# Weight halves and memory keys kept in DRAM, and one output projection for two branches

## The chip, the cores and the metric

The kernel runs on one core of one Trainium2 chip. The time is the device time of one execution in microseconds, from three runs of the kernel before. A core has TensorE (PE; its weight loads are shown as PEld), VectorE (DVE), ScalarE (ACT), GpSimd (POOL) and SyncE (SP), which issues every DMA here, in order.

## The reference

A trunk of two residual layers over 2048 tokens of width 1024, float32. Both have one combined input projection, three branches, each times a SiLU gate, and one output projection over the joined branches (512 + 512 + 256 channels):

```python
z = xn @ w_in                       # xn = rms_norm(h, norm_g[layer])
# layer 0 (even): A chunked spatial gating | B multi-scale pooling | M memory attention
# layer 1 (odd):  C window attention       | D convolution module  | M memory attention
y = concatenate([ya, yb, ym], axis=-1) @ w_out_even   # odd: [yc, yd, ym] @ w_out_odd
h = h + y
```

Branch M attends from every token to 256 memory tokens, whose keys and values depend on the layer alone.

## The kernel before

The tokens are four blocks of 512 (`TB`), channels on the 128 partitions. Each block passes the even layer and then the odd one: eight stages, in the order even 0, even 1, odd 0, even 2, odd 1, even 3, odd 2, odd 3. Between the layers the residual rows lie in DRAM (`h1`).

Every float32 matrix product is three matmuls (`mm3`, L125): each factor is split into a high half, rounded to the PE's fast format, and a low half, the rest. `hi_of` (L119) is a copy on ACT, `lo_of` (L122) a subtraction on DVE or POOL; all of them show as L120 and L123, and the tile's name tells which: `wh`, `wl` weights, `xnh`, `xnl` the normalised input, `yh`, `yl` the branch outputs, `km` memory keys, `q` queries, `kt` window keys.

`wslot` (L137) brings 128x1024 weights: SP loads the raw tile (two buffers), ACT makes `wh`, POOL or DVE `wl` (four buffers each). `share` gives DVE every third low half in even stages and none in odd ones. A unit of the input projection (`proj`, L322) is one slot and 24 matmuls. This is done anew in each stage: a weight of a layer is loaded and split four times.

`load_mem` (L427) loads the memory keys in each stage and stacks them (`stack_keys`, L297: four copies on ACT, four low halves on DVE, into `km`). `finish` (L330) splits a branch output, the low half on DVE. `out_steps` (L504) multiplies finished outputs with output weights, one 128-channel unit at a time, and DVE adds each unit to the residual row (L521), which frees the PSUM bank. It is called for the first branch (offset 0, four inputs, 12 matmuls a unit), the second (offset 4, the same) and the memory branch (offset 8, two inputs, 6 matmuls a unit).

`Norm` prepares the next stage's input within this one: sums of squares (`square_sum`, L160: ACT squares, DVE adds), a scale on DVE (L193), and `split`, whose low halves `xnl` DVE makes between the row adds of the last projection. In odd stages the convolution runs on DVE as 31 multiply-adds on each of four tiles (L689), put between other work. `_SEQ` (L945) lists the events of an odd stage: `S`, `V` window attention, `s`, `v` memory attention, `e` finishes branch C, `oN` runs N output units.

The order on each engine is made by a scheduler at build time, which simulates the program; on the chip each engine takes its instructions in that order.

Of the kernel before, what the change touches and what calls it, by code (L numbers as in the profile page):

```python
# [18 lines left out]
P = 128  # L19
# [33 lines left out]
def trunk(ctx: ExitStack, tc: tile.TileContext, x, mem, par, par1, wkv, w_v, w_cm0, w_kvc, w_cm1, w_o0, w_o1, awt, bw, dpw, abse, out):  # L53
# [83 lines left out]
    def wslot(src, n=1024, eng=None):  # L137
        raw = rp.tile([P, 1024], F32, tag="wr", name="wr", bufs=2)[:, :n]
        hi = wp.tile([P, 1024], F32R, tag="wh", name="wh", bufs=4)[:, :n]
        lo = wp.tile([P, 1024], F32R, tag="wl", name="wl", bufs=4)[:, :n]  # L140
        nc.sync.dma_start(raw, src)
        hi_of(hi, raw)
        turns[0] += 1
        lo_of(eng or (V if turns[0] % share[0] == 0 else G), lo, raw, hi)
        return hi, lo
# [14 lines left out]
    def square_sum(srcs, n_buf=1):  # L160
        bufs = []
        for _ in range((n_buf + 2) // 2):
            t = p_tile().rearrange("p a b -> p (a b)")
            bufs += [t[:, :TB], t[:, TB:]]
        total, bufs = bufs[0], bufs[1:]
        for i, src in enumerate(srcs):
            sq = bufs[i % n_buf] if i else total
            A.activation(sq, src, AF.Square)
            if i:
                V.tensor_tensor(total, total, sq, op=ALU.add)  # L170
        return total, bufs[0]
# [40 lines left out]
    mkv = [tc.dram_tile([2, P, TB], F32, name=f"mkv{l}") for l in range(2)]  # L212
# [46 lines left out]
    def prep_mem(memt):  # L259
        for l in range(2):  # L260
            gm = sb.tile([P, P], F32, tag="kn", name="kn", bufs=2)[:, :64]
            V.tensor_tensor(gm, par_of(f"mq{l}"), par_of(f"mk{l}"), op=ALU.mult)
            kv = sb.tile([P, 2, 2, 256], F32, tag="pt", name="kv", bufs=2)
            for hf in range(2):
                ws = [view(wslot(wkv[l, hf, q]), "p (k n) -> p k n", k=4) for q in range(2)]
                for mt in range(2):
                    pb = mm_bank()[:, :256]
                    ms = slice(mt * P, (mt + 1) * P)
                    for k in range(KC):
                        wh, wl = ws[k // 4]  # L270
                        mm3(pb, memt[0][k // 4][:, k % 4, ms], memt[1][k // 4][:, k % 4, ms],
                            wh[:, k % 4, :], wl[:, k % 4, :], k == 0, k == KC - 1)
                    if hf:
                        A.copy(kv[:, 1, mt, :], pb)
                    else:
                        mem_keys(gm, mt, pb, kv[:, 0])
            nc.sync.dma_start(mkv[l].rearrange("a p m -> p a m"), kv.rearrange("p a b m -> p a (b m)"))
# [44 lines left out]
    def proj(xn, w_cm, unit):  # L322
        wh, wl = view(wslot(w_cm[unit]), "p (k c) -> p k c", k=KC)
        pb = mm_bank()
        for k in range(KC):
            mm3(pb, wh[:, k, :], wl[:, k, :], xn[0][:, k, :], xn[1][:, k, :], k == 0, k == KC - 1)
        pump(2)
        return pb

    def finish(y):  # L330
        hi = half("yh", 4, F32R)
        lo = half("yl", 4, F32R)
        done[0] = hi_of(hi, y)
        lo_of(V, lo, y, hi)
# [92 lines left out]
    def load_mem(l):  # L427
        km = sb.tile([P, 4, 2, 256], F32R, tag="km", name="km", bufs=1)
        vm = sb.tile([P, 2, 256], F32, tag="vm", name="vm", bufs=1)
        t = short()[:, :TB]  # L430
        nc.sync.dma_start(t, mkv[l][0])
        nc.sync.dma_start(vm.rearrange("p a b -> p (a b)"), mkv[l][1])
        stack_keys(km, t.rearrange("p (c m) -> p c m", c=2))
        return km, vm

    def memory(l, q, ys, fill):
# [10 lines left out]
        return [finish(y) for y in ys]  # L447
# [3 lines left out]
    class Norm:  # L451
# [30 lines left out]
        def split(self):  # L482
# [21 lines left out]
    def out_steps(st, first, ys):  # L504
# [94 lines left out]
    def even(st, ahead):  # L599
# [119 lines left out]
    def odd(st, ahead):  # L719
# [23 lines left out]
        cq, mq, gc, yc, ym, steps = [], [], [], [], [], []  # L743
# [47 lines left out]
        project_out(st, 8, ym)  # L791
# [6 lines left out]
        project_out(st, 4, yd)  # L798
# [109 lines left out]
    def conv_mix(st, hd, ys):  # L908
        ws = [view(wslot(dpw[q]), "p (k n) -> p k n", k=2) for q in range(2)]
# [14 lines left out]
    first_v = [wslot(w_v[0, 0], eng=G)]  # L924
    lead.measure()
    with behind(ET.DVE):
        first_v.append(wslot(w_v[0, 1], eng=V))
    first_v = [view(w, "p (k n) -> p k n", k=4) for w in first_v]
    xn = lead.scale_split()
    for n, (is_odd, b) in enumerate(order):  # L930
# [15 lines left out]
        "s1 o2 v0 s2 v1 o2 s3 v2 o2 v3")  # L946
# [30 lines left out]
def _lay_out(i):  # L977
# [12 lines left out]
    for n, w in (("w_o0", i["w_out_even"][0]), ("w_o1", i["w_out_odd"][0][rows1])):  # L990
        a[n] = np.concatenate([_out_slots(w[P * k:P * (k + m)], m) for k, m in ((0, 4), (4, 4), (8, 2))])
# [53 lines left out]
```

## Time and profile before

| | us |
|---|---|
| median of three runs (1968.65 to 1969.47) | 1969.15 |
| the profiled execution | 1970.85 |
| its span, first to last instruction | 1968.9 |
| PE busy | 1899.1 |
| DVE busy | 1374.2 |
| POOL busy | 872.8 |
| ACT busy | 825.3 |

The profiled execution has 1.95 us around its span. A busy time is a share of the whole span; what an engine holds up is read from the waits and from stretches of single stages. "Idle before" tells what ended the wait of an engine; matmuls overlap, so a stretch of them is read from the starts.

### The profile page before, as it was taken

To read this page: it belongs to the slowest core of one execution; us is meant where nothing else is said; L and a number is where in the kernel's file an instruction comes from. 1 tells how busy PE (TensorE), PEld (TensorE's weight loads), DVE (VectorE), ACT (ScalarE), POOL (GpSimd) and SP (SyncE) were. 2 spreads that over 40 slices of the span, in tenths; PEclk is the share of its full clock that TensorE was granted. 3 is DMA by queue.
4 is the path that set the end of the run, shared out by engine and by line. 5 is a ranking of instruction groups with operands and counts; after the bars stand their busy time and mean duration, and the time that the engine had idled before them with its cause. 6 is when DMAs were issued, how large, how long until landed. Compare 5 with 4: busy or idle time off the path is not lost.

```text
span 1968.9 us, 26523 instructions
## 1 busy us (share of the span) xinstructions
PE 1899.1 (96%) x10034; PEld 1569.0 (80%) x10034; DVE 1374.2 (70%) x2262; ACT 825.3 (42%) x1663; POOL 872.8 (44%) x593
## 2 busy tenths in 40 slices
PE   6999999999998999999999899999999989999999
PEld 6878888787886878878788687988878767888687
DVE  6776544645999673565699967355569986699954
ACT  4453324423355442442435443353333544435532
POOL 3672225323555443623445443453245544445542
PEclk9999999999999999999999999999999999999999
DMA  5443353334322334232532233432252223532122
GB/s 207 152 137 113 102 173 106 109 99 166 97 86 70 103 107 160 96 113 86 177 97 67 68 124 132 136 113 97 86 178 86 75 66 111 166 108 71 59 76 75
DMA packets 61440, 218.96 MB, mean 111 GB/s; under 512 B 6785, under 2 KB 6913, under 8 KB 61185
## 3 DMA queue, kind: packets, MB, share of 16 engines
q1 hardware_dynamic: 61312, 217.27, 33.9%
q8 instruction: 79, 1.29, 0.3%
q14 instruction: 49, 0.39, 0.1%
HBM read 198.63 MB, written 18.61 MB: 110 GB/s over the span
## 4 chain that ended last, share of the span: by engine, by line
PE 47%; DVE 9%; ACT 1%; issue 0%; DMA 0%; POOL 0%; ACTq 0%; POOLq 0%; SPq 0%
PE mm L126 12%; PE mm L127 12%; PE mm L128 12%; DVE cv L689 3%; PE cv L128 2%; PE cv L126 2%; PE cv L127 2%; DVE xnl L123 1%; PE pv L417 1%; PE tr L385 1%; PE tr L312 1%; PE tr L313 1%; DVE row L521 1%; PE pv L357 1%; DVE pt L853 1%; DVE q L123 0%
## 5 line engine op out<-in xcount | busy, mean ns | idle before, releaser
L123 POOL TENSOR_TENSOR wl<-wr,wh 128x1024 fp32r<-128x1024 f32 (+1 forms) x250 | 606.6, 2428 | 866.6 <-ACT wh L120 808.2
L120 ACT CAST wh<-wr 128x1024 fp32r<-128x1024 f32 (+1 forms) x300 | 312.6, 1042 | 655.0 <-PE mm L127 358.6
L126 PE MATMUL mm<-xnh,wh 128*128 128x512 f32 x1176 | 464.3, 395 | 0.4 <-ACT u L354 0.4
L128 PE MATMUL mm<-xnh,wl 128*128 128x512 f32 x1176 | 461.6, 393 | 0.2 <-DVE wl L123 0.2
L127 PE MATMUL mm<-xnl,wh 128*128 128x512 f32 x1176 | 460.7, 392 | 0.0
L689 DVE SCALAR_TENSOR_TENSOR cv<-hx,dwh,cv 128x512 f32<-128x512 f32 x464 | 349.0, 752 | 9.1
L128 PEld LDWEIGHTS mm<-xnh,wl 128*128 128x128 f32 x1176 | 221.3, 188 | 47.2 <-issue 1.2
L127 PEld LDWEIGHTS mm<-xnl,wh 128*128 128x128 f32 x1176 | 221.6, 188 | 45.9 <-issue 2.8
L126 PEld LDWEIGHTS mm<-xnh,wh 128*128 128x128 f32 x1176 | 221.4, 188 | 44.0 <-issue 0.6
L126 PE MATMUL mm<-yh,wh 128*128 128x512 f32 x534 | 215.5, 406 | 23.8 <-DVE row L521 14.4
L127 PE MATMUL mm<-yl,wh 128*128 128x512 f32 x534 | 210.6, 394 | 1.1 <-DVE yl L123 1.1
L128 PE MATMUL mm<-yh,wl 128*128 128x512 f32 x534 | 210.5, 394 | 0.0
L521 DVE TENSOR_TENSOR row<-mm,row 128x512 f32<-128x512 f32 x160 | 109.1, 686 | 122.9 <-PE mm L128 122.6
L126 PEld LDWEIGHTS mm<-yh,wh 128*128 128x128 f32 x534 | 100.9, 190 | 56.3 <-DVE row L521 23.1
L127 PEld LDWEIGHTS mm<-yl,wh 128*128 128x128 f32 x534 | 101.0, 189 | 21.6 <-DVE yl L123 2.0
L128 PEld LDWEIGHTS mm<-yh,wl 128*128 128x128 f32 x534 | 100.9, 189 | 21.4 <-issue 0.2
L123 DVE TENSOR_TENSOR wl<-wr,wh 128x1024 fp32r<-128x1024 f32 (+1 forms) x50 | 66.3, 1326 | 68.8 <-ACT wh L120 68.7
L403 ACT ACTIVATE p<-tr,mnb,qm 128x256 f32<-128x256 f32 x128 | 70.6, 561 | 69.6 <-DVE mnb L400 65.1
L377 POOL TENSOR_SCALAR p<-p,mrd 128x256 f32<-128x256 f32 x128 | 64.1, 521 | 79.5 <-DVE mrd L406 78.4
L126 PE MATMUL mm<-wh,xnh 128*128 128x256 f32 x320 | 91.8, 287 | 2.9 <-ACT xnh L120 1.8
L128 PE MATMUL mm<-wh,xnl 128*128 128x256 f32 x320 | 91.0, 285 | 1.3 <-DVE xnl L123 1.1
L126 PE MATMUL cv<-xnh,wh 128*128 128x512 f32 x232 | 92.1, 397 | 0.0
(226 smaller groups left out, 3378.3 us busy)
## 6 DMA issues: line engine op xcount, KB each, us to landing
wr<-in_w_cm_dram SPq DMA_DIRECT2D x176, 512.0 KB, 3.5
wr<-in_w_o_dram SPq DMA_DIRECT2D x80, 512.0 KB, 3.5
wr<-in_w_v_dram SPq DMA_DIRECT2D x16, 512.0 KB, 3.5
row<-in_x_dram SPq DMA_DIRECT2D x16, 512.0 KB, 4.1
h<-row SPq DMA_DIRECT2D x16, 512.0 KB, 3.5
row<-h SPq DMA_DIRECT2D x16, 512.0 KB, 3.9
out_dram<-row SPq DMA_DIRECT2D x15, 512.0 KB, 2.7
x<-in_x_dram SPq DMA_DIRECT2D x8, 512.0 KB, 3.6
```

What stands on the lines that cost most here:

```text
L120: return A.copy(hi, raw)
L123: eng.tensor_tensor(lo, raw, hi.bitcast(F32), op=ALU.subtract)
L126: T.matmul(out, lhsT=lh, rhs=rh, start=first, stop=False)
L127: T.matmul(out, lhsT=lh, rhs=rl, start=False, stop=False)
L128: T.matmul(out, lhsT=ll, rhs=rh, start=False, stop=last)
L312: T.matmul(out, lhsT=q[g][:, cols], rhs=keys[:, g], start=True, stop=False)
L313: T.matmul(out, lhsT=q[g][:, cols], rhs=keys[:, 2 + g], start=False, stop=True)
L357: T.matmul(sp[:, 2 * tt:2 * tt + 2], lhsT=sq[:, tt * P:(tt + 1) * P], rhs=par_of("bones"), start=True, stop=True)
L377: G.tensor_scalar(p[:, h, :], p[:, h, :], rd[:, h:h + 1], 1.0, op0=ALU.mult, op1=ALU.mult)
L403: A.activation(p[:, h, :], banks[h // 2][:, (h % 2) * 256:(h % 2) * 256 + 256], AF.Exp, bias=nb[:, h:h + 1], scale=qr[:, tt, h:h + 1], acc ...
L521: add = V.tensor_tensor(row, pb, row, op=ALU.add)
L689: V.scalar_tensor_tensor(dst, src, w, acc, op0=ALU.mult, op1=ALU.add)
```

## The change

`wslot` takes a key. At a key's first use it loads and splits as before, into one tile `w` that holds both halves (four buffers), and SP stores that tile in DRAM. At the second to fourth use SP loads both halves from there (1 MB) and nothing is split. Only the weights of the memory keys and values have no key: they are used once. The stacked keys are made and stored once per layer (`mkey`), and `load_mem` only loads them (1 MB). The low halves in `finish` and `split`, and the adds of `square_sum` (but for the first one of the program), go from DVE to POOL. The memory branch's outputs join the second branch's projection: six inputs, 18 matmuls a unit, slots of 768 columns with one unit each; the projection at offset 8 is gone. In odd stages `_SEQ` has one output unit where it had two, and those left over run after the convolution's norm.

```diff
@@ -134,14 +134,22 @@
 
-    def wslot(src, n=1024, eng=None):
+    halves = {}
+
+    def wslot(src, n=1024, eng=None, key=None):
+        w = wp.tile([P, 2, 1024], F32R, tag="w", name="w", bufs=4)[:, :, :n]
+        hi, lo = w[:, 0], w[:, 1]
+        if key in halves:
+            nc.sync.dma_start(w.bitcast(F32), halves[key])
+            return hi, lo
         raw = rp.tile([P, 1024], F32, tag="wr", name="wr", bufs=2)[:, :n]
-        hi = wp.tile([P, 1024], F32R, tag="wh", name="wh", bufs=4)[:, :n]
-        lo = wp.tile([P, 1024], F32R, tag="wl", name="wl", bufs=4)[:, :n]
         nc.sync.dma_start(raw, src)
...
         lo_of(eng or (V if turns[0] % share[0] == 0 else G), lo, raw, hi)
+        if key:
+            halves[key] = tc.dram_tile([P, 2, n], F32, name="w_" + "_".join(map(str, key)))
+            nc.sync.dma_start(halves[key], w.bitcast(F32))
         return hi, lo
...
@@ -167,7 +175,7 @@
             if i:
-                V.tensor_tensor(total, total, sq, op=ALU.add)
+                (V if n_buf > 1 else G).tensor_tensor(total, total, sq, op=ALU.add)
         return total, bufs[0]
...
@@ -209,7 +217,8 @@
     vtail = const.tile([P, P], F32, name="vtail")
-    mkv = [tc.dram_tile([2, P, TB], F32, name=f"mkv{l}") for l in range(2)]
+    mkey = [tc.dram_tile([P, 4, 2, 256], F32, name=f"mkey{l}") for l in range(2)]
+    mval = [tc.dram_tile([P, TB], F32, name=f"mval{l}") for l in range(2)]
 
...
@@ -274,7 +283,10 @@
                         mem_keys(gm, mt, pb, kv[:, 0])
-            nc.sync.dma_start(mkv[l].rearrange("a p m -> p a m"), kv.rearrange("p a b m -> p a (b m)"))
+            km = sb.tile([P, 4, 2, 256], F32R, tag="km", name="km", bufs=1)
+            stack_keys(km, kv[:, 0])
+            nc.sync.dma_start(mkey[l], km.bitcast(F32))
+            nc.sync.dma_start(mval[l], kv[:, 1].rearrange("p b m -> p (b m)"))
 
...
@@ -320,7 +332,7 @@
     def proj(xn, w_cm, unit):
-        wh, wl = view(wslot(w_cm[unit]), "p (k c) -> p k c", k=KC)
+        wh, wl = view(wslot(w_cm[unit], key=("cm", int(w_cm is w_cm1), unit)), "p (k c) -> p k c", k=KC)
         pb = mm_bank()
...
@@ -328,10 +340,10 @@
     def finish(y):
-        hi = half("yh", 4, F32R)
-        lo = half("yl", 4, F32R)
+        hi = half("yh", 6, F32R)
+        lo = half("yl", 6, F32R)
         done[0] = hi_of(hi, y)
-        lo_of(V, lo, y, hi)
+        lo_of(G, lo, y, hi)
         return hi, lo
...
@@ -427,10 +439,8 @@
         vm = sb.tile([P, 2, 256], F32, tag="vm", name="vm", bufs=1)
-        t = short()[:, :TB]
-        nc.sync.dma_start(t, mkv[l][0])
-        nc.sync.dma_start(vm.rearrange("p a b -> p (a b)"), mkv[l][1])
-        stack_keys(km, t.rearrange("p (c m) -> p c m", c=2))
+        nc.sync.dma_start(km.bitcast(F32), mkey[l])
+        nc.sync.dma_start(vm.rearrange("p a b -> p (a b)"), mval[l])
         return km, vm
...
@@ -485,7 +494,7 @@
                 hi_of(xn[0][:, k, :], self.xs[k])
-                lo_of(V, xn[1][:, k, :], self.xs[k], xn[0][:, k, :])
+                lo_of(G, xn[1][:, k, :], self.xs[k], xn[0][:, k, :])
             rate[0] = 3
...
@@ -506,12 +515,13 @@
         per = KC // n
+        size = per * n * P
         ws = {}
...
             if q not in ws:
-                ws[q] = view(wslot(w_o[first + q]), "p (u k n) -> p u k n", u=per, k=n)
+                ws[q] = view(wslot(w_o[first + q, :, :size], size, key=("o", int(st["odd"]), first + q)), "p (u k n) -> p u k n", u=per, k=n)
             wh, wl = ws[q]
...
@@ -633,14 +643,12 @@
         df = [None] * 4
-        ym = memory(0, q, gm, lambda tt: pool_windows(st, df, tt))
+        memory(0, q, gm, lambda tt: pool_windows(st, df, tt))
         nx = ahead()
-        wb = view(wslot(bw, TB), "p (g d) -> p g d", g=4)
-        yb = [pool_map(st, g, df[g], wb) for g in range(3)]
-        project_out(st, 8, ym)
-        yb.append(pool_map(st, 3, df[3], wb))
+        wb = view(wslot(bw, TB, key=("bw",)), "p (g d) -> p g d", g=4)
+        yb = [pool_map(st, g, df[g], wb) for g in range(4)]
+        steps = out_steps(st, 4, yb + [finish(y) for y in gm])
         ya = [sgu(st, 0, xhs, wt, abias)]
-        steps = out_steps(st, 4, yb)
         for f in steps[:4]:
...
@@ -788,14 +793,16 @@
         hd = conv_swish(st, xhs)
-        project_out(st, 8, ym)
+        for f in steps:
+            f()
+        ym = [finish(y) for y in gm]
         if nx:
...
             st["next"] = nx.split()
-        project_out(st, 4, yd)
+        project_out(st, 4, yd + ym)
         flush()
...
@@ -943,7 +950,7 @@
 _SEQ = ("f6 q S0 g2 S1 g2 V0 f1 S2 V1 f1 S3 V2 f2 s0 V3 f2 e "
-        "s1 o2 v0 s2 v1 o2 s3 v2 o2 v3")
+        "s1 o1 v0 s2 v1 o1 s3 v2 o1 v3")
 _TC = dict(schedule_with_timeline_sim=True)
...
@@ -988,7 +995,7 @@
     for n, w in (("w_o0", i["w_out_even"][0]), ("w_o1", i["w_out_odd"][0][rows1])):
-        a[n] = np.concatenate([_out_slots(w[P * k:P * (k + m)], m) for k, m in ((0, 4), (4, 4), (8, 2))])
+        a[n] = np.concatenate([_out_slots(w[P * k:P * (k + m)], m) for k, m in ((0, 4), (4, 6))])
     a["awt"] = i["a_ws"][0].transpose(2, 0, 1)
...
     a["dpw"] = _tm_slots(i["d_pw"][0], 2)

...
```

VectorE at the end of stage even 2, from the last projection's first row add on (`row`) to the next stage; before, then now:

```order
L521 TENSOR_TENSOR row<-cv,row 128x512
L123 TENSOR_TENSOR xnl<-x,xnh 128x512 x3
L521 TENSOR_TENSOR row<-mm,row 128x512
L123 TENSOR_TENSOR xnl<-x,xnh 128x512
L123 TENSOR_TENSOR xnl<-p,xnh 128x512 x2
L521 TENSOR_TENSOR row<-mm,row 128x512
L123 TENSOR_TENSOR xnl<-p,xnh 128x512 x2
L521 TENSOR_TENSOR row<-cv,row 128x512
L521 TENSOR_TENSOR row<-mm,row 128x512 x2
L521 TENSOR_TENSOR row<-cv,row 128x512
```

```order
L602 TENSOR_TENSOR gt<-u_7894,gt 128x512
L604 SCALAR_TENSOR_TENSOR gt<-cv,gt 128x512
L531 TENSOR_TENSOR row<-mm,row 128x512 x2
L531 TENSOR_TENSOR row<-cv,row 128x512
L531 TENSOR_TENSOR row<-mm,row 128x512 x2
L531 TENSOR_TENSOR row<-cv,row 128x512
L531 TENSOR_TENSOR row<-mm,row 128x512 x2
```

The eight low halves `xnl` have left DVE, and its row adds follow each other. They stand on POOL now, behind the four `yl` of the first branch (`krsb` and `qc` are the next stage's):

```order
L123 TENSOR_TENSOR yl<-gt,yh 128x512 x4
L123 TENSOR_TENSOR xnl<-x,xnh 128x512 x4
L123 TENSOR_TENSOR xnl<-p,xnh 128x512 x4
L165 TENSOR_TENSOR krsb<-krsa,nhalf 128x2 x4
L373 TENSOR_TENSOR qc<-qss,nhalf 128x8 x4
```

GpSimd at the end of the attention of stage odd 1 (`qm` query scales, `p<-p,mrd` the weighing of a memory tile); before, then now:

```order
L361 TENSOR_TENSOR qm<-qss,nhalf 128x8
L123 TENSOR_TENSOR wl<-wr,wh 128x1024
L361 TENSOR_TENSOR qm<-qss,nhalf 128x8
L377 TENSOR_SCALAR p<-p,mrd 128x256 x8
L123 TENSOR_TENSOR wl<-wr,wh 128x1024
L377 TENSOR_SCALAR p<-p,mrd 128x256 x4
L123 TENSOR_TENSOR wl<-wr,wh 128x1024
L377 TENSOR_SCALAR p<-p,mrd 128x256 x4
```

```order
L373 TENSOR_TENSOR qm<-qss,nhalf 128x8
L862 AFFINE_SELECT pt<-pt 128x512
L373 TENSOR_TENSOR qm<-qss,nhalf 128x8
L389 TENSOR_SCALAR p<-p,mrd 128x256 x4
L123 TENSOR_TENSOR yl<-gt,yh 128x512 x4
L389 TENSOR_SCALAR p<-p,mrd 128x256 x12
L178 TENSOR_TENSOR p<-p 128x512
L123 TENSOR_TENSOR yl<-gt,yh 128x512 x2
```

The `wl` rows are gone in this stage, and the four `yl` of branch C stand behind the first weighing and ahead of the other three.

SyncE in stage even 0, from the pooling weights on; before, then now:

```order
L141 DMA wr_1438<-in_bw_dram 128x512
L277 DMA mkv1_106<-kv_853 128x2x512
L141 DMA wr_1444<-in_w_cm0_dram 128x1024
L141 DMA wr_1492<-in_w_cm0_dram 128x1024
L141 DMA wr_1540<-in_w_cm0_dram 128x1024
L141 DMA wr_1588<-in_w_o0_dram 128x1024
```

```order
L146 DMA wr_1448<-in_bw_dram 128x512
L288 DMA mkey1_106<-km_1022 128x2048
L152 DMA w_cm_0_11_1358<-w_1353 128x2048
L146 DMA wr_1455<-in_w_cm0_dram 128x1024
L152 DMA w_bw_1452<-w_1447 256x1x512
L146 DMA wr_1504<-in_w_cm0_dram 128x1024
L442 DMA km_1043<-mkey0_105 128x2048
L152 DMA w_cm_0_12_1459<-w_1454 128x2048
L146 DMA wr_1553<-in_w_cm0_dram 128x1024
L152 DMA w_cm_0_13_1508<-w_1503 128x2048
```

The store of a slot's halves stands between the raw loads, and the reload of the stacked keys behind the second layer's store of them.

## Rows read from the trace of the kernel before

**Rows 1.** The page's first lines: busy us, share of the span, instructions of an engine
```profile
span 1968.9 us, 26523 instructions
...
PE 1899.1 (96%) x10034; PEld 1569.0 (80%) x10034; DVE 1374.2 (70%) x2262; ACT 825.3 (42%) x1663; POOL 872.8 (44%) x593
```

**Rows 2.** TensorE's rate, timeline: start us, duration us; one 24-matmul unit
```profile
500.08 0.39 PE L126 MATMUL mm<-xnh,wh 128*128 128x512 f32 x1
...
505.53 0.39 PE L126 MATMUL mm<-xnh,wh 128*128 128x512 f32 x1
```

**Rows 3.** Waits of TensorE: engine, line, releaser: us in total, times, longest
```profile
PE mm L126 <- DVE row L521: 15.7, 17, 1.6
PE tr L179 <- DVE p L170: 11.1, 1, 11.1
PE mm L126 <- ACT yh L120: 8.5, 4, 3.9
PE pv L862 <- DVE pt L853: 5.0, 3, 2.3
PE tr L714 <- DVE kn L711: 3.7, 5, 0.9
```

**Rows 4.** Granted clock of the core over the span
```profile
core 0: 1968.9 us, clock 0.995
```

**Rows 5.** Four stretches, one per odd stage: us, busy us of each engine, clock, DMA
```profile
600.00:650.00 50.00, 43.91 (x222) 32.00 (x221) 48.58 (x95) 26.92 (x75) 25.38 (x23) 0.93 0.18 58
1075.00:1125.00 50.00, 43.09 (x212) 32.25 (x209) 48.38 (x100) 28.90 (x78) 24.64 (x21) 0.93 0.24 79
1575.00:1600.00 25.00, 19.75 (x91) 14.10 (x89) 22.14 (x41) 9.85 (x26) 11.65 (x9) 0.86 0.16 45
1825.00:1875.00 50.00, 45.39 (x234) 34.77 (x234) 49.15 (x96) 27.20 (x72) 26.09 (x24) 1.00 0.20 64
```

**Rows 6.** Timeline at an even stage's end: VectorE, then TensorE
```profile
945.95 4.09 DVE L123 TENSOR_TENSOR xnl<-x,xnh 128x512 fp32r<-128x512 f32 x3
949.96 0.68 DVE L521 TENSOR_TENSOR row<-mm,row 128x512 f32<-128x512 f32 x1
...
950.69 0.50 PE L126 MATMUL mm<-yh,wh 128*128 128x512 f32 x1 [1.52 <-DVE row L521]
```

**Rows 7.** VectorE's groups by shape: count, busy us, mean ns, idle before
```profile
L521 DVE TENSOR_TENSOR row<-mm,row 128x512 f32<-128x512 f32 x160 | 109.1, 686 | 122.9 <-PE mm L128 122.6
L123 DVE TENSOR_TENSOR yl<-gt,yh 128x512 fp32r<-128x512 f32 x80 | 66.3, 845 | 12.3 <-ACT yh L120 12.3
...
L123 DVE TENSOR_TENSOR km<-u,km 64x512 fp32r<-64x512 f32 x32 | 42.5, 1328 | 2.9 <-ACT km L300 2.2
```

**Rows 8.** Timeline at the end of an odd stage's attention: VectorE, ScalarE, GpSimd, TensorE
```profile
1113.39 3.12 DVE L689 SCALAR_TENSOR_TENSOR cv<-hx,dwh,cv 128x512 f32<-128x512 f32 x4
1116.42 0.15 DVE L400 SCALAR_TENSOR_TENSOR mnb<-mmx,qm 128x4 f32<-128x4 f32 x1
...
1118.79 2.17 ACT L120 CAST yh<-gt 128x512 fp32r<-128x512 f32 x4
...
1119.21 1.85 POOL L377 TENSOR_SCALAR p<-p,mrd 128x256 f32<-128x256 f32 x4 [3.06 <-DVE mrd L406]
...
1119.46 1.22 PE L126 MATMUL mm<-yh,wh 128*128 128x512 f32 x2 [3.91 <-ACT yh L120]
```

**Rows 9.** One line on VectorE: duration ns min/median/max, first and last start
```profile
L123 DVE TENSOR_TENSOR yl<-gt,yh x80: 675/686/2546, 149.3 to 1944.3; 128x512 fp32r<-128x512 f32 x80
```

**Rows 10.** GpSimd's low halves of weights by shape, columns as in rows 7
```profile
L123 POOL TENSOR_TENSOR wl<-wr,wh 128x1024 fp32r<-128x1024 f32 x248 | 604.0, 2437 | 857.5 <-ACT wh L120 799.1 <-PE mm L128 24.3 <-ACT pt L387 11.8
...
L123 POOL TENSOR_TENSOR wl<-wr,wh 128x512 fp32r<-128x512 f32 x2 | 2.6, 1292 | 9.1 <-ACT wh L120 9.1
```

**Rows 11.** ScalarE's high halves of weights, columns as in rows 7
```profile
L120 ACT CAST wh<-wr 128x1024 fp32r<-128x1024 f32 x296 | 310.1, 1048 | 651.2 <-PE mm L127 358.6 <-issue 110.2 <-PE cv L127 66.7
```

**Rows 12.** Issue of weights on SyncE (KB each, us to landing); all loads of L141
```profile
wr<-in_w_cm_dram SPq DMA_DIRECT2D x176, 512.0 KB, 3.5
...
DMA to landing us min/median/max: 2.5/3.5/7.6
```

**Rows 13.** DMA of 0 to 25 us: GB/s in 40 slices
```profile
GB/s 0 0 26 151 249 413 420 406 393 419 413 407 414 413 419 419 439 426 419 419 341 0 0 105 242 387 105 52 85 341 397 432 407 380 351 436 413 426 419 406
```

More of the change, by code (lines that the diff above doesn't have):

```diff
@@ L446, in memory @@
                 fill(tt)
-        return [finish(y) for y in ys]
     paced, rate, done = [], [1], [None]
@@ L609, in even @@
                 with behind(ET.DVE):
-                    ws = [view(wslot(w_v[hf, j]), "p (k n) -> p k n", k=4) for j in range(2)]
+                    ws = [view(wslot(w_v[hf, j], key=("v", hf, j)), "p (k n) -> p k n", k=4) for j in range(2)]
             for tt in range(NT):
@@ L693, in keys @@
         xn, kt, va = st["xn"], st["kt"], st["va"]
-        ws = [view(wslot(w_kvc[q]), "p (k n) -> p k n", k=4) for q in range(2)]
+        ws = [view(wslot(w_kvc[q], key=("kvc", q)), "p (k n) -> p k n", k=4) for q in range(2)]
         for tt in range(NT):
@@ L742, in odd @@
         km, vm = load_mem(1)
-        cq, mq, gc, yc, ym, steps = [], [], [], [], [], []
+        cq, mq, gc, yc, steps = [], [], [], [], []
         pc, pm = {}, {}
@@ L779, in odd @@
         run(len(fills))
-        for f in steps:
-            f()
-        ym = [finish(y) for y in gm]
         gd = [gate(st, w_cm1, 16 + u) for u in range(3)]
@@ L908, in conv_mix @@
     def conv_mix(st, hd, ys):
-        ws = [view(wslot(dpw[q]), "p (k n) -> p k n", k=2) for q in range(2)]
+        ws = [view(wslot(dpw[q], key=("dpw", q)), "p (k n) -> p k n", k=2) for q in range(2)]
         for u in range(4):
@@ L923, in trunk @@
     nc.sync.dma_start(pc, par)
-    first_v = [wslot(w_v[0, 0], eng=G)]
+    first_v = [wslot(w_v[0, 0], eng=G, key=("v", 0, 0))]
     lead.measure()
     with behind(ET.DVE):
-        first_v.append(wslot(w_v[0, 1], eng=V))
+        first_v.append(wslot(w_v[0, 1], eng=V, key=("v", 0, 1)))
     first_v = [view(w, "p (k n) -> p k n", k=4) for w in first_v]
@@ L964, in _out_slots @@
     per = KC // n
-    v = w.reshape(n, P, n, per, P).transpose(2, 1, 3, 0, 4)
-    return np.ascontiguousarray(v).reshape(n, P, D)
+    v = w.reshape(n, P, KC // per, per, P).transpose(2, 1, 3, 0, 4).reshape(KC // per, P, per * n * P)
+    return np.pad(v, ((0, 0), (0, 0), (0, D - v.shape[2])))
 def _chan(v):
```

## The prediction

> **What bounds the kernel.** I read the busy lines first: TensorE works 1899.1 of 1968.9 us, VectorE 1374.2, GpSimd 872.8, ScalarE 825.3 [rows 1]. TensorE is the bound, and 69.8 us is all that it stands idle. Its rate comes from the timeline: a unit of 24 matmuls starts 5.45 us before the next, 227 ns a matmul [rows 2]. The change leaves the matmul work as it is, since two inputs of the memory branch are moved from a projection of their own into another. So of the 500 us of work that it removes elsewhere, only what TensorE waits for counts, and what makes its matmuls slower.
>
> The waits come second [rows 3]: 15.7 us in 17 waits for VectorE's row add, 11.1 at the start, 8.5 for ScalarE's `yh`, 3.7 for key halves, 5.0 for the window attention's `pt`. The clock third: 0.995 over the span [rows 4], so some 0.005 x 1968.9 = 9.8 us are lost at half clock. Fourth, where: one stretch of each odd stage, at the end of its attention [rows 5]. TensorE is idle there for 6.1, 6.9, 5.25 and 4.6 us, 22.9 in all, while VectorE is busy 97, 97, 89 and 98%; three of the four have clocks of 0.93, 0.93 and 0.86, which makes 3.5 + 3.5 + 3.5 us, all the clock's loss. It falls to its lower level, 1.2 GHz, right after these waits.
>
> **The change, part by part.** All sums are made against the profiled execution, 1970.85 us (1.95 around the span), which is 1.7 above the median of 1969.15.
>
> *Row waits at stage ends.* In the timeline three `xnl` stand ahead of a row add on VectorE for 4.09 us, and TensorE waits 1.52 us for the bank that the add frees [rows 6]. The change moves all `xnl` to GpSimd (the first order piece), so the adds follow each other, and a unit becomes 18 matmuls, 18 x 0.227 = 4.1 us, for one add of 0.686 [rows 7]. What is late next is the matmul itself. Of the 15.7 us I take 15, between 10 (some of the 17 waits are for adds behind other work) and 15.7: **-15**.
>
> GpSimd has the eight `xnl` instead: 8 x 1.292 (the 128x512 low half there, the nearest row [rows 10]) = 10.3 us, and four `yl` of 5.2 ahead. The last projection of an even stage covers 8 units x 12 matmuls x 0.227 = 21.8 us, of an odd one 32.7. Hidden. Without that cover it is 15.5 us a stage at most.
>
> *Keys.* 24 of 32 `km` low halves, 1.33 us each [rows 7], leave VectorE, where they stand ahead of the key norms that TensorE waits 3.7 us for: **-3**, between 0 and -3.7.
>
> *End of the odd stages' attention.* In the timeline four taps of 3.12 us hold `mnb` back, GpSimd waits 3.06 us for what follows from it, the branch's gate is late, ScalarE's `yh` with it, and TensorE waits 3.91 us [rows 8]. The change takes work off VectorE in every stage: 64 row adds x 0.686 = 44, 80 `yl` = 66, 24 `km` = 32 us by [rows 7], and at some 0.8 us each 56 `xnl`, about 52 square sums and 34 `wl`: some 270 of 1374. The taps stay, and `_SEQ` has one projection unit where it had two, so that units are left to fill TensorE later. I take half of the 22.9 us: **-11**, between 0 and -20. With fewer gaps half of the clock's 9.8 us goes: **-5**, between 0 and -9.8.
>
> *`yl` on GpSimd.* It is 1.29 us in place of 0.69 (the minimum on VectorE [rows 9]), and the first may stand behind a weighing of 4 x 256, 1.85 us [rows 8] (the second piece on GpSimd shows it behind the first of four weighings). TensorE takes one input for two banks in 6 matmuls, 1.36 us, so the four keep pace after the first: **+2**, between 0 (covered by ready matmuls) and 16 finishing places x 2.5 us = 40 (four at 1.29 last 5.2 us, at 0.69 they last 2.7).
>
> *No splitting in six stages.* ScalarE loses some 215 casts of 1.05 us [rows 11], GpSimd about 185 low halves of 2.44 and gains `yl`, `xnl` and sums: 873 becomes some 650. TensorE hardly waits for these halves now, so I count **0**, from 0 to -5. VectorE also loses neighbours: a `yl` took 675 ns at best and 2546 at worst [rows 9], while a `wl` on GpSimd lasts 2437 [rows 10]. The Trainium skill ("SBUF — State Buffer", section "Who interferes with whom") says that VectorE with two inputs from SBUF is kept out while GpSimd reads there; the longest `yl` agrees. By that rule each piece moved to GpSimd blocks in its turn, so the work taken off VectorE is worth less than its sum. I have halved the odd stretches' gain already, from the rows.
>
> *Loads of both halves.* A slot of 512 KB lands in 3.5 us [rows 12]. For 1 MB I bound it by 4.75 (the second 524 KB at 420 GB/s, near the peak of [rows 13], is 1.25 us) and 7.0 (twice); I take 6. There are four buffers, and a load starts when a slot is left, three slots ahead: 16 us, or 10.9 while the pooling weights hold one. The need is 1.049 MB in 5.45 us, 192 GB/s, under half of 420. **0**. What hides it is TensorE's own work; below 10.9 us nothing shows.
>
> *First use.* In even 0 and odd 0 SP issues the raw load of slot j + 2 behind the store of slot j, which waits for its low half (the SP piece). The raw buffer made the same load wait for the same low half before, so the period of two slots is landing + cast + low half = 3.5 + 1.05 + 2.44 = 7.0 us, 3.5 a slot against 5.45. **0** in the running part. In even 0 the first keys come by a chain: stacking, which takes some 8 us of VectorE and ScalarE, then the store and the reload at some 5 each, 18 us, against 96 matmuls = 21.8 us that are ready. With 3 us to spare I charge **+3**, between 0 and +10.
>
> Sum: -15 - 3 - 11 - 5 + 2 + 3 = -29, so 1942 by the profiled run and **1940** by the median. Terms at their better ends, with -5 for the halves, give -54, about 1915; at their worse ends (-10 + 0 + 0 + 0 + 10, and +10 for `yl`, a quarter of its bound) +10.
>
> **The rivals.**
>
> *Deeper.* VectorE, 20% lighter, stops being late at all, and all waits but the start and the end go: -69.8 + 11.1 + 3.6 (the rest after the last matmul, an estimate) = -55, and the clock's 9.8 partly: -60, **1909**. For it: VectorE stands behind most of the waits. Against: `pt` waits (5.0) are in the window attention's own chain, and the taps stay.
>
> *Small gain.* Only the row waits shrink, and the odd stretches wait as long, since the chain of the gate and the taps holds: between -4 and -13, **1960**.
>
> *No change.* The idle 3.5% forms again behind other releasers: GpSimd's `yl` in place of VectorE's row adds. A change within 0.2%, 3.9 us, can't be told from none by a measurement of this kernel: **1968**.
>
> *Slower: the store in SP's queue.* In the first-use stages a load stands behind a store in a queue that is served in order. The raw loads run beside stores of 1 MB then, and their landing stretches. The point is where (landing + 3.5) / 2 passes 5.45: at 7.4 us; 7.6 was the longest [rows 12]. At 8.5 us each of the 77 stored slots would cost 6.0 - 5.45 = 0.55 us: +42, and with -29 that is **1982**. For it: traffic doubles, and a first-use slot moves 0.524 in and 1.049 out in 5.45 us, 288 GB/s, with the 45 to 79 of stretches with few weights [rows 5] some 350. Against: up to 439 GB/s were moved at the start [rows 13], which leaves a fifth.
> The Trainium skill ("DMA: Bandwidth & Descriptors", section "Specifications") gives about 358 GB/s as a core's share of HBM; the slices at 413 to 439 speak against that as a ceiling here. By that figure some 2% would be left and this rival would be likelier.
>
> *Slower, too:* GpSimd, in order, gives each of the 16 finishing places the whole 2.5 us: -29 + 40 = +11, **1980**. Or the 1 MB loads come at 175 GB/s when spread over the stage, below the need of 192: 6.0 us a slot in place of 5.45, on some 230 slots, +125.
>
> **How the numbers follow.** Forecast (1922 to 1956) 0.58; deeper 0.12; small gain 0.09; no change 0.08; slower 0.13 (0.06 for the store, 0.04 for `yl`, 0.03 for the loads). Faster: 0.58 + 0.12 + 0.09 = 0.79. The range runs from 1908, the deeper case, to 1966, the end of the small gain; outside lie the slower cases, part of no change, and a tail below. The likeliest case by itself: 1922 to 1956.
>
> **What would show it.** Right: in the page after, TensorE's busy time near 1895 and idle time near 40; its waits for the row add under 2 us in all; the four odd stretches with half of the idle time, and a clock above 0.997; 1 MB loads that land in 5 to 7 us and no wait of TensorE that a DMA ended outside the first stage. The first-use step is right if raw loads still land under 7.4 us in even 0 and odd 0, and the key chain if TensorE waits no more than 3 us before its first scores. Wrong: waits of TensorE for GpSimd's `yl` or `xnl` above 5 us in all (then the low halves on GpSimd are the bound at stage ends); waits at slots' starts at regular distances of a unit (then loads are); or a TensorE busy time that moves by more than 15 us with the matmuls unchanged, which none of my terms has but the clock.

## The result, and the profile after

The changed kernel takes **1949.56 us** (median of four runs, 1947.57 to 1952.3), before 1968.9 in the same runs: a ratio of 0.9898, 95% interval 0.9885 to 0.9910. That is 19.3 us faster where 29 were forecast. The profiled execution has a span of 1950.6 us. The page's first lines after, beside [rows 1]:

```profile
span 1950.6 us, 25978 instructions
...
PE 1894.8 (97%) x10034; PEld 1572.1 (81%) x10034; DVE 1039.7 (53%) x1952; ACT 601.3 (31%) x1424; POOL 659.8 (34%) x600
```

VectorE lost 335 us of busy time, ScalarE 224, GpSimd 213, and the span 18.3 us. TensorE's idle time went from 69.8 to 55.8 us and its busy time from 1899.1 to 1894.8. The waits of TensorE after, beside [rows 3]:

```profile
PE tr L187 <- DVE p L178: 11.2, 1, 11.2
PE mm L126 <- ACT yh L120: 10.4, 4, 3.1
PE tr L187 <- POOL p L178: 4.0, 1, 4.0
PE mm L126 <- DVE gt L354: 3.0, 1, 3.0
...
PE mm L127 <- POOL w L123: 2.0, 1, 2.0
...
PE tr L722 <- DVE kn L719: 1.6, 3, 1.2
...
PE mm L127 <- POOL yl L123: 1.1, 2, 0.6
...
PE mm L126 <- DVE row L531: 0.9, 1, 0.9
```

The row waits are gone, 15.7 to 0.9; `yh` at the end of the odd attention stayed, 8.5 to 10.4; new are 4.0 for a square sum of GpSimd and 3.0 for a gate. The clock over the span did not rise (before, [rows 4]). In the four stretches that answer to [rows 5], each placed around its wait for `yh`, TensorE is idle for 3.7, 4.3, 3.6 and 3.45 us, 15.0 in all:

```profile
core 0: 1950.6 us, clock 0.994
```

```profile
596.00:646.00 50.00, 46.31 (x226) 34.88 (x225) 47.53 (x94) 27.36 (x75) 30.85 (x28) 0.97 0.52 184
1069.00:1119.00 50.00, 45.67 (x240) 34.00 (x240) 47.49 (x101) 24.35 (x74) 17.65 (x20) 1.00 0.35 122
1556.00:1581.00 25.00, 21.44 (x116) 15.79 (x115) 23.68 (x50) 12.20 (x36) 7.83 (x9) 1.00 0.37 127
1805.00:1855.00 50.00, 46.55 (x241) 35.60 (x241) 47.10 (x99) 25.30 (x79) 18.66 (x23) 0.93 0.30 105
```

The clock of 1.00 in the third row is not a gain: the fall comes just behind that stretch, with 0.82 from 1581 to 1600 us. Two falls are in places that had none before: 0.72 from 96 to 102 us in even 0, and 0.72 from 697 to 703 us in odd 0, behind the wait of 4.0 us for the sum.

The timeline of such an end, beside [rows 8], shows why the wait stayed:

```profile
1107.35 2.33 DVE L697 SCALAR_TENSOR_TENSOR cv<-hx,dwh,cv 128x512 f32<-128x512 f32 x3
...
1107.58 1.94 PE L869 MATMUL pv<-pt,va 128*64 128x512 f32 x8 [0.30 <-DVE qss L372]
...
1109.59 0.16 DVE L412 SCALAR_TENSOR_TENSOR mnb<-mmx,qm 128x4 f32<-128x4 f32 x1
...
1109.66 0.88 DVE L877 SCALAR_TENSOR_TENSOR gt<-pv,gt 128x128 f32<-128x128 f32 x4
1109.78 0.56 ACT L415 ACTIVATE p<-tr,mnb,qm 128x256 f32<-128x256 f32 x1 [3.64 <-DVE mnb L412]
...
1111.97 2.17 ACT L120 CAST yh<-gt 128x512 fp32r<-128x512 f32 x4
...
1112.64 0.73 PE L126 MATMUL mm<-yh,w 128*128 128x512 f32 x2 [3.12 <-ACT yh L120]
```

VectorE's gate `gt` follows the window product `pv` at once now and is done at 1110.5. But four exponentials of the memory attention stand ahead of `yh` on ScalarE until 1111.97, and they begin late: they wait 3.64 us for `mnb`, which VectorE makes behind three taps of the convolution, where it made it behind four before. TensorE has no other matmul ahead of the one that waits.

The loads and stores, from the page's DMA issues (count, KB, median us to landing). A load of both halves (`w<-w_cm`, 1 MB) takes 4.9 us, the store of a slot 4.8, and a raw load at the first use 6.1 where it took 3.5 [rows 12]:

```profile
w<-w_cm SPq DMA_DIRECT2D x132, 1024.0 KB, 4.9
w_cm<-w SPq DMA_DIRECT2D x44, 1024.0 KB, 4.8
...
wr<-in_w_cm_dram SPq DMA_DIRECT2D x44, 512.0 KB, 6.1
```

These are medians: 8 of the 85 raw loads took more than 7.4 us, up to 9.8, and the 12 loads of `w_v` halves had a median of 8.4 and a longest of 13.3.

To see where time went, I worked out TensorE's **lost time** in each stage, from the traces. It is the time between the last row adds of two stages, less the time that the TensorE instructions begun in it need. Each of these is counted with the median step from start to start that its kind had in the kernel before (227 ns for a 512-column matmul; 1843.1 us in all, the same in every kernel). The rows of the table are kernels of the experiments below; a row with a plus has that part beside the kept halves. The tail after the last row add is 3.6 to 4.1 us.

```
us lost in       even0 even1 odd0  even2 odd1  even3 odd2  odd3  median run
before            30.0   8.2  17.9  10.7  17.6   7.0  18.7  12.1   1969
halves kept only  28.5   6.6  12.3   3.0  11.4   3.0  10.8  10.8   1934.9
 + keys kept      42.9   6.9  14.5   3.4   9.8   3.4  11.6  11.5   1953.4
 + join           27.7   6.6  17.3   3.0  11.3   3.0  11.1   8.5   1937.7
 + GpSimd moves   28.7   3.2  17.0   3.2  12.0   3.2  10.8  10.6   1939.5
 + keys, join     32.5   6.9  16.4   3.4   9.9   3.3  10.2  10.0   1942.4
the change        32.9   3.4  23.9   4.3   9.2   4.8  13.1  12.3   1949.6
```

The change gains 27.2 us in the six stages that load halves and gives 8.9 back in the two that fill the copies in DRAM: 2.9 in even 0 and 6.0 in odd 0. Each row is one execution. That of the change is the longest of its four, 2.7 us above the median, and the granted clock of the four goes from 0.992 to 0.995. So a difference of 2 or 3 us in a single stage decides nothing.

### The profile page after: what moved, and what is told of

Its sections match the earlier page's. It is cut to its first block, busy times and chain, and to the rows that moved or that the text cites. A ratio compares the mean times of both kernels' runs of the same rounds, so it can differ in the third digit from the quotient of the medians.

```text
span 1950.6 us, 25978 instructions
## 1 busy us (share of the span) xinstructions
PE 1894.8 (97%) x10034; PEld 1572.1 (81%) x10034; DVE 1039.7 (53%) x1952; ACT 601.3 (31%) x1424; POOL 659.8 (34%) x600
## 4 chain that ended last, share of the span: by engine, by line
PE 87%; DMA 5%; DVE 3%; POOL 2%; ACT 2%; issue 1%; SPq 0%; ACTq 0%; POOLq 0%; DVEq 0%
PE mm L126 21%; PE mm L127 21%; PE mm L128 21%; PE cv L126 4%; PE cv L128 4%; PE cv L127 4%; DMA out_dram<-row 2%; PE tr L324 2%; PE pv L429 2%; PE tr L325 2%; PE tr L397 1%; POOL w L123 1%; PE pv L869 1%; PE pv L369 1%; PE pv L594 1%
## 5 line engine op out<-in xcount | busy, mean ns | idle before, releaser
L126 PE MATMUL mm<-xnh,w 128*128 128x512 f32 x1184 | 468.3, 396 | 0.4 <-ACT u L366 0.4
L128 PE MATMUL mm<-xnh,w 128*128 128x512 f32 x1184 | 464.0, 392 | 1.6 <-POOL w L123 1.6
L127 PE MATMUL mm<-xnl,w 128*128 128x512 f32 x1184 | 463.5, 391 | 0.0
L128 PEld LDWEIGHTS mm<-xnh,w 128*128 128x128 f32 x1184 | 222.3, 188 | 49.0 <-POOL w L123 2.0
L126 PEld LDWEIGHTS mm<-xnh,w 128*128 128x128 f32 x1184 | 222.6, 188 | 45.1 <-issue 1.5
L127 PEld LDWEIGHTS mm<-xnl,w 128*128 128x128 f32 x1184 | 222.6, 188 | 43.2 <-issue 0.7
L126 PE MATMUL mm<-yh,w 128*128 128x512 f32 x536 | 210.8, 397 | 13.5 <-ACT yh L120 10.4
L127 PE MATMUL mm<-yl,w 128*128 128x512 f32 x536 | 211.9, 395 | 1.1 <-POOL yl L123 1.1
L128 PE MATMUL mm<-yh,w 128*128 128x512 f32 x536 | 210.9, 394 | 0.0
L123 POOL TENSOR_TENSOR w<-wr,w 128x1024 fp32r<-128x1024 f32 (+1 forms) x69 | 158.2, 2295 | 134.7 <-ACT w L120 131.5
L123 POOL TENSOR_TENSOR yl<-gt,yh 128x512 fp32r<-128x512 f32 x80 | 104.6, 1321 | 257.3 <-ACT yh L120 257.3
L126 PEld LDWEIGHTS mm<-yh,w 128*128 128x128 f32 x536 | 101.6, 190 | 39.5 <-ACT yh L120 13.9
L127 PEld LDWEIGHTS mm<-yl,w 128*128 128x128 f32 x536 | 101.8, 190 | 23.2 <-POOL yl L123 2.1
L128 PEld LDWEIGHTS mm<-yh,w 128*128 128x128 f32 x536 | 101.6, 190 | 21.0 <-POOL w L123 0.2
```

Source lines behind the costliest of these rows:

```text
L123: eng.tensor_tensor(lo, raw, hi.bitcast(F32), op=ALU.subtract)
L126: T.matmul(out, lhsT=lh, rhs=rh, start=first, stop=False)
L127: T.matmul(out, lhsT=lh, rhs=rl, start=False, stop=False)
L128: T.matmul(out, lhsT=ll, rhs=rh, start=False, stop=last)
```

## The experiments

Each was timed in five rounds; ratios are to the kernel before in the same rounds.

**One move undone: `xnl`.** In `split`, `lo_of(G, xn[1]...)` is `lo_of(V, ...)` again (V is VectorE, G GpSimd).

> The changed kernel with one line put back: the low halves xnl of the next stage's input are made on VectorE again. Theory A (the gain is the row waits at the stage ends, and they went because xnl left VectorE): the waits for row come back, 11 to 16 us of them, time 1949.6 + 12 = about 1961. Theory B (they went because nothing is split in those stages: three xnl took 4.09 us beside GpSimd's weight halves, alone they take 3 x 0.69 = 2.1, less than the 2.7 us of a 12-matmul unit): row waits stay under 3 us, time within 3 us of 1949.6. Theory C (joining the projections did it): as B in odd stages, as A in even ones, about 1957.

1950.5 us, ratio 0.9904 (0.9890 to 0.9918): no difference from the change. Theory A, my prediction's, falls: row waits of 15 us did not come back (3.2 in three, two of them in even 1). With the kept halves they stay away, whichever engine makes `xnl`.

**The join undone.** `project_out(st, 8, ym)`, two output units per event and the old order of the odd stage's end again.

> The changed kernel with the join undone: the memory branch has its own projection of 6-matmul units again (offset 8), the order string two output units per event, and the remaining units run before the convolution's norm, as before the change. Theories A and B, in which the join is worth little: 64 more row adds of 0.69 us on an engine that works half of the time; a unit of 6 matmuls lasts 1.36 us against an add of 0.69, so no wait; within 4 us of 1949.6. Theory C: the odd stages lose what they gained (some 17 us of the 19 lie in odd 1 and odd 2), time about 1965.

1956.9, 0.9938 (0.9925 to 0.9950). Slower by 7, outside what A and B allowed and not where theory C had it: the lost time of odd 1 and odd 2 is as with the join (10.1 and 13.0), even 0 loses 46.1 in place of 32.9, and odd 0 loses 15.5 in place of 23.9. The keys explain even 0, below; odd 0 stays open.

**Splitting in each stage.**

```diff
-        if key:
+        if False:
             halves[key] = ...
```

> The changed kernel without the store of weight halves: each stage loads the raw weights and splits them again, as before the change, with the low halves of weights on GpSimd beside yl, xnl and the sums, which stay there; the stacked keys stay in DRAM. GpSimd has then 660 + 447 = about 1110 us. Theory A (what counts is that VectorE is relieved, keeping halves is worth nothing by itself): within 6 us of 1949.6, since the first two stages keep their cost. Theory B (the splitting hurts, by GpSimd's queue or by VectorE's slower operations): the sums and low halves on GpSimd are late behind weights in every stage as they are now in odd 0 (7 us of waits there): 6 stages x 3 to 7 us, 1968 to 1990.

1983.7, 1.0076 (1.0062 to 1.0090), as theory B had it: all the rest of the change without the kept halves is *slower* than the kernel before. TensorE's wait for key halves grows to 13.8 us in five, and the timeline shows its chain in odd 2: the roots `krsb` for the window keys `kn` stand behind a weight half on GpSimd. VectorE's `krsa` ahead of them, two operations of 128x2, took 2.06 us beside that half.

```profile
1449.12 2.34 POOL L123 TENSOR_TENSOR w<-wr,w 128x1024 fp32r<-128x1024 f32 x1 [0.84 <-ACT w L120]
1451.56 1.36 POOL L165 TENSOR_TENSOR krsb<-krsa,nhalf 128x2 f32<-128x2 f32 x2
```

```profile
1452.82 0.48 PE L722 MATMUL tr<-ident,kn 128*128 128x128 f32 x1 [5.22 <-DVE kn L719]
```

**Sums back on VectorE.** `V.tensor_tensor(total, ...)` in `square_sum`.

> The changed kernel with the seven adds of each square sum on VectorE again. In odd 0 TensorE waits 4.0 us for a sum of GpSimd (which makes weight halves there too) and 3.0 us for a gate behind GpSimd's root. If the sums on GpSimd are what odd 0 lost: those 4.0 us go, and perhaps the 3.0, nothing comes elsewhere: 1943 to 1946. If VectorE then holds up the row adds or the taps: 1950 or more.

1947.3, 0.9880 (0.9865 to 0.9895), 2 us better, with the intervals overlapping and between the two ranges expected. The 4.0 us went, but the gate's wait in odd 0 rose from 3.0 to 5.9: that stage's lost time fell only from 23.9 to 22.2.

**The kept halves alone**, put into the kernel before (the new `wslot` and its keys, nothing else).

> The kernel before with one part of the change alone: weight halves are stored at first use and loaded at the later ones. The stacking of keys in each stage, the placement of low halves and sums on VectorE, the two projections and the order string stay as before the change. Theory B (keeping the halves is what pays: xnl and the chains of the odd stages are no longer beside or behind GpSimd's weight halves): the row waits at the even stages' ends fall under 3 us; most of the gain is there, 1969.6 - 12 = about 1957, the rest being the join (7 us by the run with two projections). Theory D (the keeping pays only since low halves and sums were moved to GpSimd, where weights would delay them): nothing to 4 us, 1966 to 1970.

**1934.9**, 0.9823 (0.9810 to 0.9837): 34.7 us faster than before, where 12 were expected, and 14.6 faster than the whole change. This run shows the mechanism at the ends of even stages, with and without its cause. At the end of even 2 odd 1's halves are loaded; at the end of even 1 odd 0's weights are split for the first time. VectorE in even 2, where GpSimd runs nothing from 925 to 946 us:

```profile
932.82 1.89 DVE L123 TENSOR_TENSOR xnl<-x,xnh 128x512 fp32r<-128x512 f32 x3
934.63 0.68 DVE L529 TENSOR_TENSOR row<-mm,row 128x512 f32<-128x512 f32 x1
```

and VectorE, then GpSimd, in even 1:

```profile
459.82 4.08 DVE L123 TENSOR_TENSOR xnl<-x,xnh 128x512 fp32r<-128x512 f32 x3
463.83 0.68 DVE L529 TENSOR_TENSOR row<-mm,row 128x512 f32<-128x512 f32 x1
```

```profile
460.79 2.56 POOL L123 TENSOR_TENSOR w<-wr,w 128x1024 fp32r<-128x1024 f32 x1 [54.44 <-ACT w L120]
```

The same three operations take 1.89 us alone and 4.08 beside one weight half. In [rows 6] they took 4.09, and GpSimd had a weight half there too:

```profile
946.74 2.75 POOL L123 TENSOR_TENSOR wl<-wr,wh 128x1024 fp32r<-128x1024 f32 x1 [5.06 <-ACT wh L120]
```

A 12-matmul unit lasts 2.7 us: only the slow ones make TensorE wait for row adds, 2.9 us in even 1 and nothing in even 2. Even 2 loses 3.0 us where it lost 10.7.

More of the gain lies in the odd stages: odd 0 to odd 3 lose 21.0 us less, even 1 to even 3 13.3. VectorE splits no weights in odd stages, so its instructions there are the same in both kernels. Its busy time (the third of the engines' numbers in a row) in odd 0 and odd 1, before and with the halves kept:

```profile
480.70:745.70 265.00, 256.69 (x1312) 208.65 (x1310) 216.71 (x388) 121.73 (x275) 123.48 (x83) 0.99 0.31 102
963.40:1231.10 267.70, 257.99 (x1336) 212.12 (x1336) 219.20 (x388) 123.07 (x277) 127.21 (x84) 0.99 0.32 105
```

```profile
478.20:740.40 262.20, 255.87 (x1335) 209.51 (x1335) 212.24 (x388) 119.53 (x273) 120.34 (x82) 1.00 0.73 257
947.70:1209.00 261.30, 257.05 (x1335) 212.11 (x1334) 200.10 (x387) 86.11 (x238) 36.59 (x47) 0.99 0.53 186
```

In odd 1, where GpSimd lost its weight halves, the same work of VectorE takes 19.1 us less; in odd 0, where it still splits them, 4.5 less. How much of the odd stages' gain comes from this, how much from GpSimd's shorter queue and how much from ScalarE's (its casts of weights went too, 123.1 to 86.1 us in odd 1), no run separates.

**All moves to GpSimd undone**, with keys and join: `V` in `finish`, `split` and `square_sum`.

> The changed kernel with all that went to GpSimd put back on VectorE: yl, xnl and the sums. Halves and keys kept, projections joined. Theory B: these moves are worth nothing or cost a little (odd 0: 4 us for a sum, 3 us for a root behind GpSimd's work): 1943 to 1950. Theory A': moved work must go to GpSimd for the taps and the odd stages to be on time: 1955 or more.

1942.4, 0.9863 (0.9849 to 0.9876), just under theory B's range: the moves cost 7.2 us, and most of it lies in odd 0 (23.9 to 16.4). One such place in the changed kernel's trace, GpSimd and then TensorE: between the sums stand weight halves of odd 0, and the last sum comes 4 us late.

```profile
687.53 1.32 POOL L178 TENSOR_TENSOR p<-p 128x512 f32<-128x512 f32 x1
689.59 1.29 POOL L178 TENSOR_TENSOR p<-p 128x512 f32<-128x512 f32 x1 [0.75 <-DMA wr<-in_w_o_dram]
690.83 1.85 POOL L123 TENSOR_TENSOR w<-wr,w 128x768 fp32r<-128x768 f32 x1
692.64 1.28 POOL L178 TENSOR_TENSOR p<-p 128x512 f32<-128x512 f32 x1
694.44 1.80 POOL L123 TENSOR_TENSOR w<-wr,w 128x768 fp32r<-128x768 f32 x1 [0.52 <-ACT w L120]
696.19 1.26 POOL L178 TENSOR_TENSOR p<-p 128x512 f32<-128x512 f32 x1
```

```profile
697.51 0.72 PE L187 MATMUL tr<-ones,p 128*128 128x2 f32 x5 [4.02 <-POOL p L178]
```

**The other moves into the kept halves.** Each of these three adds one part to the 1934.9 kernel: the keys kept, the join with its order string, the moves to GpSimd.

> The kernel before with the weight halves kept (1934.9 us) and the stacked keys kept as well; nothing moved to GpSimd, two projections. If the keys are what the first stage lost: even 0 is 3 to 4 us slower (stack, store and reload, and casts that stand ahead of weights), the three later stages of each layer gain at most 1 us each: 1934 to 1939. If not: 1930 to 1934.

> The kernel before with the weight halves kept and the projections joined, with the change's order string; keys stacked in each stage, nothing moved to GpSimd. With both kept halves and kept keys the joined kernel takes 1942.4. If the join costs the 7.5 us between that and 1934.9: 1940 to 1943. If the keys do: 1934 to 1938.

> The kernel before with the weight halves kept and yl, xnl and the sums moved to GpSimd; two projections, keys stacked in each stage. From the pair with the join (1949.6 with the moves, 1942.4 without) the moves cost 7 us: 1940 to 1945, and most of it lies in odd 0, where GpSimd splits weights as well. With two projections even 0 had lost 13 us beside the moves (1956.9 with keys kept): if that was the moves' doing, 1948 to 1957.

Keys 1953.4, 0.9916 (0.9901 to 0.9932), **18.5 us slower**; join 1937.7, 0.9838 (0.9821 to 0.9854), slower by 2.8 with overlapping intervals; moves 1939.5, 0.9844 (0.9829 to 0.9859), 4.5 slower, most of it in odd 0 (12.3 to 17.0), the intervals overlapping. The expectation for the keys was wrong by a factor of four: 14.4 us are lost in even 0. The tile `km` on TensorE (count, ns, first and last start), with the halves alone and with the keys too:

```profile
L320 PE MATMUL tr<-km,q x128: 276/281/415, 105.8 to 1843.9; 128*128 128x256 f32 x128
```

```profile
L324 PE MATMUL tr<-km,q x128: 276/281/415, 132.2 to 1861.6; 128*128 128x256 f32 x128
```

The first memory scores start 26 us later. SP's rows of that kernel say why: the reload of the first layer's keys stands behind the second layer's store, which waits until the second layer's keys are stacked.

```profile
113.76 0.32 SPq L288 DMA_DIRECT2D mkey<-km  x1
119.53 1.73 SPq L442 DMA_DIRECT2D km<-mkey  x1
```

The queue is not all that holds it. `km` has one buffer: both layers' keys are stacked in it one after the other, and the reload writes to it again. So in the order that the kernel is written in, the reload has to come after the second store in any queue; whether another order would cure it was not tried.

By then the projection units that lay beside the memory attention are used up, and it runs alone, with TensorE waiting at many steps:

```profile
154.44 1.80 PE L397 MATMUL tr<-ident,p 128*128 128x128 f32 x8 [0.56 <-POOL p L389]
158.69 1.19 PE L429 MATMUL pv<-pt,vm 128*64 128x128 f32 x16 [2.45 <-ACT pt L399]
```

From 94 to 164 us the granted clock is 0.93 here and 1.00 with the halves alone, which makes some 5 of the 14.4 us. Joined, the memory outputs are wanted later, and the same delay costs 4.8 (27.7 to 32.5). So the join is worth 11 us beside the keys and nothing without them: it covers a delay that the change itself brings. The run with the join undone lost 13.2 us in even 0 in the same way.

**A projection unit held back** until the last window product of an odd stage, so that TensorE has work while `yh` is made.

```diff
-        for k in range(KC):
-            mm3(pb, wh[:, k, :], wl[:, k, :], xn[0][:, k, :], xn[1][:, k, :], k == 0, k == KC - 1)
+        with tc.issue_after(held[0]) if held[0] else nullcontext():
+            for k in range(KC):
+                mm3(pb, wh[:, k, :], wl[:, k, :], xn[0][:, k, :], xn[1][:, k, :], k == 0, k == KC - 1)
...
-_SEQ = ("f6 q S0 g2 S1 g2 V0 f1 S2 V1 f1 S3 V2 f2 s0 V3 f2 e "
+_SEQ = ("f6 q S0 g2 S1 g2 V0 f1 S2 V1 f1 S3 V2 f2 s0 f1 V3 F1 e "
```

In `_SEQ`, `fN` runs N units of the input projection, and the new event `F1` runs one with `held` set to the last window product, so that its matmuls start after it.

> The changed kernel with one unit of the input projection (24 matmuls, 5.45 us) held until the last window-attention product of an odd stage is done, and the branch's finish behind it. TensorE waits there now 3.1 us in three stages and 1.06 in odd 0 for yh, whose chain is product, gate on VectorE 0.9, four exponentials on ScalarE that stand ahead, cast. If the wait is there because nothing else is queued, it goes: -10 us, and up to 8 more if the half-clock stretches behind it (3.4 and 6.8 us) go too: 1932 to 1941. If the unit only leaves another hole ahead of that product (its pt chain of some 3 us is no longer covered): 1947 to 1953.

> The held projection unit together with yl, xnl and the sums back on VectorE. If both effects are separate, their sum: some 3 us below the run with the held unit alone.

> The kernel before with the weight halves kept and the held projection unit at the end of the odd stages' attention. With the whole change the held unit gave 11.6 us. If the waits for yh (10.6 us here) go in the same way: 1923 to 1928, the quickest version. If the unit ahead of the last window product was needed here: 1930 or more.

In the changed kernel 1938.0, 0.9839 (0.9826 to 0.9853), 11.6 better, as expected of the waits alone; with all moves undone as well 1939.5, 0.9848 (0.9834 to 0.9861), not below that: the two effects don't add up, and why stays open. In the kernel with halves alone 1935.9, 0.9829 (0.9814 to 0.9844): nothing. There the waits for `yh` went (idle time 45.2 to 37.6), but busy time rose from 1888.3 to 1897.0 at a clock of 0.992 in place of 0.996. In odd 1 the clock had fallen to its lower level, 1.2 GHz, before the window product, after a run of short transposes and products with waits of 0.2 to 0.9 us. The product, and the stretch around it with its granted clock (the third number from the end), with halves alone:

```profile
1093.47 1.94 PE L870 MATMUL pv<-pt,va 128*64 128x512 f32 x8 [0.60 <-DVE qss L368]
```

```profile
1088.00:1099.00 11.00, 7.22 (x43) 5.37 (x42) 10.68 (x24) 3.97 (x13) 4.58 (x5) 0.94 0.28 95
```

and with the unit held:

```profile
1092.42 3.68 PE L876 MATMUL pv<-pt,va 128*64 128x512 f32 x8 [0.35 <-DVE qss L370]
```

```profile
1088.00:1099.00 11.00, 10.45 (x33) 6.76 (x33) 9.54 (x23) 4.36 (x12) 4.28 (x5) 0.53 0.00 0
```

Without the hold that unit lies ahead of the product. That its absence there lets the clock fall was not tried by itself; in the changed kernel with the held unit the clock did not fall there (1.00 from 1085 to 1110 us). No run beat the kept halves alone: 1934.9 is the quickest, and the held unit with them can't be told from it.

## Why the prediction was right or wrong

The sign, the range and the bound (TensorE, 97% after) were right; the ledger behind them was not. By the runs the change is made up of -34.7 for the kept halves, +7.5 for the keys and the join, and +7.2 for the moves to GpSimd, -20.0 in all, as the medians of different rounds add up. That 29 was forecast and 19.3 came is in part luck: the largest gain stood at 0 in the sum, and most of what it counted as gains of the moves was the halves' doing.

**"No splitting in six stages: 0, from 0 to -5" is the step that failed.** Alone it measured -34.7. I had read that TensorE hardly waits for weight halves, which is so, and had not followed what they do to others. VectorE's low halves last twice as long beside them, and GpSimd's small operations queue behind them: roots are seen to hold TensorE up in the run that splits in each stage. [Rows 6] and [rows 9] held the price: three `xnl` in 4.09 us where the minimum of the like `yl` is 0.675. The Trainium skill's rule that I cited there ("SBUF — State Buffer", section "Who interferes with whom") agrees with 1.89 against 4.08; I used it against the change, where it spoke for it. The row adds, which read one input from PSUM, didn't suffer from `xnl` on GpSimd: 690 ns after, 686 before. VectorE also lost more than I summed up, 335 us against some 270 (the terms as listed make 256): operations that stayed there got shorter too, such as the 16 `gt<-u,gt`, from 1574 to 731 ns on the mean.

**"Row waits -15"**: 14.8 came, by a wrong cause; the run with `xnl` back on VectorE has the same time. Only in even 1, where weights are still split, is the move worth some 3 us.

**"End of the odd stages' attention -11, clock -5"**: the idle time of those stretches fell by 8, the wait for `yh` not at all. The gate no longer waits behind the taps, but `mnb` does, and with it the four exponentials that stand ahead of `yh` on ScalarE. The clock gave back nothing over the span (0.995 and 0.994): what odd 1 gained there was lost to the new falls in even 0, odd 0 and odd 3.

**"Keys -3" and "+3" in even 0**: the waits for window keys went from 3.7 to 1.6, a gain of 2.1. The chain of store and reload cost 4.8 with the join and 14.4 without. From the first layer's store (93.1 us in the run with keys kept) to the first scores it is 39 us, where I had counted two transfers: the other layer's stacking and store come between, and the order shown for SP had that in it.

**"`yl` on GpSimd +2"**: `yl` itself cost nothing (1.1 us of waits before and after). The moves together cost 7.2 in the changed kernel, and 4.5 beside the halves alone, where the intervals overlap. The waits that show are for sums and a gate in odd 0, a stage that I had priced at 0; but undoing the sums alone gave only 2, so how the cost divides among the moves stays open.

**The rivals.** The store in SP's queue did not decide: raw loads stretched to a median of 6.1 us, under 7.4, though 8 of 85 passed it, and TensorE waited some 5 us for first-use weights. Most 1 MB loads landed in 4.9 us. Two waits of TensorE hung on loads, in even 3 and odd 3, 2.5 us in all, where I had said that none would outside the first stage. The 358 GB/s that I cited from the Trainium skill ("DMA: Bandwidth & Descriptors", section "Specifications") were no ceiling here: 396 GB/s were moved from 247 to 272 us, on the mean.

## What to carry to other kernels

An engine with slack can still set the pace: price work by what it does to the operations beside and behind it, and take it away before moving other work around it. Test the parts of a change one at a time and in pairs: here one part of four brought more than the whole, one repaired another, and the first pass, which fills a cache, paid for what the later ones saved. Before putting a round trip through DRAM on a first use, read what stands ahead of the reload in the DMA queue, and what else uses the buffer that it writes.

## What had not been expected of the hardware

A kernel with less idle time was not faster, since its clock was lower: in the run with the halves alone and the unit held, TensorE was idle 7.6 us less and busy 8.7 us longer at 0.992 in place of 0.996, and eight matmuls took 3.68 us in place of 1.94.
